# A two-layer Mamba-2 and attention kernel: decay products one or two steps further on, turned x behind weights, last norm's rows on another queue

## Chip, cores, metric

The kernel runs on one core of one Trainium2 chip. The metric is the device time of one execution in microseconds (us). The core has TensorE (PE, matmuls; PEld is its weight load), VectorE (DVE), ScalarE (ACT), GpSimd (POOL), and SyncE (SP), which here only issues DMAs. Each engine works through its own instructions in the order in which they stand in the program; engines wait for each other by semaphores.

## What is computed

Two layers over 256 tokens of width 2048, in float32: a Mamba-2 (SSD) mixer and a sliding-window attention mixer, each followed by a LayerNorm of `ALPHA * x + mixer(x)`. The parts that the change touches are the SSD's diagonal term, its input, and the last norm:

```python
x_c = (xs * dt[..., None])                          # input, scaled by dt
decay_in = jnp.exp(_segsum(da))
cb = jnp.einsum("bcqgn,bcsgn->bgcqs", c_c, b_c)
y_diag = jnp.einsum("bgcqs,bgrcqs,bcsgrp->bcqgrp", cb, decay_in, x_c)
...
y = (xf - mu) * lax.rsqrt(var + EPS) * g + b        # LayerNorm, rows g and b of each layer
```

There are 64 heads in 8 groups of 8, a state of 128, chunks of 128 tokens; the attention has 32 query heads on 4 shared K/V heads.

## The kernel before, in words

**Weights and matmuls.** A float32 product is made of three matmuls in a reduced type: each weight unit (128 x 2048) is split into a high part `wh` (ScalarE, line 143) and a remainder `wl` (VectorE, line 144), and multiplied with the likewise split input `xH`, `xL` (`mac`, lines 269 to 271; `out_unit`, lines 330 to 332). Units come in halves of 512 KB through five buffers `wr`; `load_half` (line 132) issues the next half on SyncE's queue as soon as a half has been converted. `next_unit` converts some units ahead and then calls `flush`, which runs what `posts` holds.

**PSUM.** Products go to four banks `mm`, used in turn. A bank is free again when VectorE has read it: `xr` (line 337 or 339, adds an output product to the residual), `z` (line 530), `cv` (line 457), `sg` (line 980, attention gate). `ax` names four other banks for small matmuls.

**SSD layer.** Group g takes ten blocks of 128 columns: B, C, four of x, four of z (group 0 in another order). Step `10*g + b` is the place after block b of group g, and a table `plan`, filled by `at(step, function, ...)`, says what is called there. This section runs under a manual schedule: the instructions of each engine stand in the order in which the code issues them. Between the blocks stand the output units of the group before (`OUT_AT`). Per group:

- `load_decay` (SyncE, `rb`), `sum_decay` and `exp_decay` (ScalarE) make the decay tiles `e`, two of 4 heads each, `es[g, 0]` and `es[g, 1]`.
- `cb` computes C·B on TensorE (lines 539, 540), masks it into `cbm` (line 541) and multiplies both halves of `e` by it (line 544). `cbm` has one buffer.
- In group 0, `tr` turns x by TensorE and scales it into `xd` (line 560). In groups 1 to 7, `turn_blocks` turns x by blocks on VectorE into `zt` (line 574), stores it to DRAM by four DMAs (`zd`, line 577); `load_turned` reads it back as `xt` (line 585), and `scale_x` makes `xd` of it (line 593). `zt`, `xt` and the later `yz` share one buffer.
- `ymm` (line 609) multiplies `xd` with `e` on TensorE: `es[g, 0]` in its first half, `es[g, 1]` in its second.

The steps are `cb` at 10g + 4 (group 0: 9; group 1: 16), `turn_blocks` at 10g + 5, `load_turned` at 10g + 6, `scale_x` at 10g + 8, `ymm` at 10g + 9 (group 0: 11).

**Attention layer.** Stages follow `B_ORDER`: ..., gate blocks 3 (`gate_block`, last readers of `x1H` and `x1L`), output stage 2, output stage 3, which is `out_last` and computes the last norm (`done2`). In `attend`, the softmax tile `p` is turned by VectorE, stored to DRAM (`pd`, line 988) and read back as `pT` (line 1048), both on GpSimd's queue; `mask_p` makes `pm` of it (VectorE, line 1055). Here a scheduler orders the instructions of each engine. The last norm's rows `gb2` are put where `x1H` and `x1L` were, and are loaded on GpSimd's queue (lines 1109, 1110), 1 MB each as each row is spread over 128 partitions.

Of the kernel before, what the change touches and what calls it, by code (L numbers as in the profile page):

```python
# [12 lines left out]
ALU = mybir.AluOpType  # L13
AX = mybir.AxisListType

P = 128
# [46 lines left out]
def trunk(ctx: ExitStack, tc: tile.TileContext, A: dict, out: bass.AP, dbg=None):  # L63
    nc = tc.nc
# [16 lines left out]
    def nm(s):  # L81
        uid[0] += 1
        return f"{s}_{uid[0]}"
# [4 lines left out]
    def ax_tile():  # L88
        return ax_ps.tile([P, 512], F32, tag="ax", name=nm("ax"), bufs=4)
# [152 lines left out]
    posts = []  # L242

    def flush():
        fns, posts[:] = list(posts), []
        for fn in fns:
            fn()
# [221 lines left out]
    es = {}  # L469
# [42 lines left out]
    gs = [G() for _ in range(NG)]  # L512
# [20 lines left out]
    def cb(g):  # L533
        if g == 0:
            flush()
        st = gs[g]
        cbm = ap.tile([P, 384], F32, tag="cbm", name=nm("cbm"), bufs=1)
        ps = ax_tile()
        nc.tensor.matmul(ps[:, :256], st.bt[:, :128], st.ct[:], start=True, stop=True)
        nc.tensor.matmul(ps[:, 256:384], st.bt[:, 128:], st.ct[:, 128:], start=True, stop=True)  # L540
        nc.vector.tensor_tensor(cbm[:], ps[:, :384], mask_ssd, ALU.mult)
        for hf in range(2):
            e = es[g, hf]
            nc.vector.tensor_tensor(
                e[:], e[:], cbm[:].unsqueeze(1).to_broadcast([P, 4, 384]), ALU.mult
            )

    def tr(g):

# [17 lines left out]
    def turn_blocks(g):  # L567

        flush()
        st = gs[g]  # L570
        zt = ap.tile([P, 4, 2, 4, 32], F32, tag="yz", name=nm("zt"), bufs=1)
        xv = st.xs[:].rearrange("p i (c b t) -> p c b i t", c=2, b=4)
        for c in range(2):
            nc.vector.transpose(zt[:, :, c, :, :], xv[:, c, :, :, :])
        st.zd = dram.tile([4, P, 256], F32, tag="zd", name=nm("zd"), bufs=2)
        for a in range(4):
            nc.sync.dma_start(
                st.zd[a, :, :].rearrange("(b t) f -> t b f", b=4),
                zt[32 * a : 32 * a + 32, :, :, :, :].rearrange("p b c i d -> p b (c i d)"),
            )  # L580

    def load_turned(g):
        st = gs[g]
        st.xt = ap.tile([P, 2, 2, 8, 32], F32, tag="yz", name=nm("xt"), bufs=1)
        nc.sync.dma_start(st.xt[:].rearrange("p r a k d -> p (r a) (k d)"), st.zd[:].rearrange("a p f -> p a f"))

    def scale_x(g):

# [165 lines left out]
    def at(t, fn, *a):  # L754
        plan.setdefault(t, []).append((fn, *a))
# [3 lines left out]
    for g in range(NG):  # L759
        t = 10 * g  # L760
        if g == 0:
            at(3, dts.end)
            at(TD, dts.turn)
            at(TD, load_decay, 0, 1)
            at(TD, load_low, 0)
            steps = TS
            pos = dict(cb=CB0, tr=10, y=11, norm=16)
        elif g == 1:
            at(10, load_decay, 1, 0)
            at(10, load_decay, 1, 1)  # L770
            at(13, load_low, 1)
            steps = 13
            pos = dict(cb=6, zt=ZT_AT, ld=LD_AT, xd=XD_AT, y=Y_AT, norm=10 + CB_AT)
        else:
            at(t - 5, load_decay, g, 0)
            at(t - 5, load_decay, g, 1)
            at(t, load_low, g)
            steps = t - 1
            pos = dict(cb=CB_AT, zt=ZT_AT, ld=LD_AT, xd=XD_AT, y=Y_AT, norm=10 + CB_AT)
        at(steps, sum_decay, g, 0)  # L780
        at(steps + 1, exp_decay, g, 0)
        at(steps + 1, sum_decay, g, 1)
        at(steps + 2, exp_decay, g, 1)
        at(t + pos["cb"], cb, g)
        if g == 0:
            at(t + pos["tr"], tr, g)
        else:
            at(t + pos["zt"], turn_blocks, g)
            at(t + pos["ld"], load_turned, g)
            at(t + pos["xd"], scale_x, g)  # L790
        at(t + pos["y"], ymm, g)
        at(t + pos["y"], gate, g)
        at(t + pos["y"] + 2, split_y, g)
        at(t + pos["norm"], norm, g)
# [311 lines left out]
    x1_stack.close()  # L1106
    gp = pool("gp", side="right")
    gb2 = [gp.tile([P, D], F32, tag=f"gb{i}", name=f"gb2_{i}") for i in range(2)]
    nc.gpsimd.dma_start(gb2[0][:], A["lng"][1].partition_broadcast(P))
    nc.gpsimd.dma_start(gb2[1][:], A["lnb"][1].partition_broadcast(P))  # L1110
    st2 = bp.tile([P, 2, 4, 6], F32, tag="st", name="st2")

    def done2(h):
# [131 lines left out]
```

## Time and profile before

| What | Value |
|---|---|
| Median of 3 runs | 990.82 us (990.53 to 991.11) |
| The profiled execution's own time | 993.6 us |
| Its span, first to last instruction | 991.8 us |
| Mean granted TensorE clock | 0.994 |
| DMA, over the span | 218.72 MB, mean 221 GB/s |
| Weight loads `wr` on SyncE's queue | 322 of 512 KB |

A row of the timeline gives the start in us, the duration, the engine, the line, the operation, the tiles (out<-in) and a count of merged instructions; in brackets stands the idle time of the engine before it, and what ended it. A granted clock of 0.50 means that TensorE runs at half rate.

### The profile page before, as it was taken

The page shows a single profiled execution, that of the slowest core. Times are in us where ns is not written, and L with a number is a line of the kernel's source. Part 1 is how long each engine was busy: PE and PEld are TensorE (multiplying, and loading weights), DVE is VectorE, ACT ScalarE, POOL GpSimd, SP SyncE. Part 2 cuts the span into 40 slices and gives each one's busy share as a digit, 9 for nine tenths or more (in the row PEclk, how much of TensorE's full clock was granted, in tenths as well). Part 3 has the DMA queues.
Part 4 walks back from the last instruction along what each step waited for, and adds up shares of the span by engine and source line. Part 5 has one row for each costly group of instructions (what it writes and reads, how often), then busy time and mean ns, then how long its engine had stood idle before and what let it go on. Part 6 is the DMA issues. An engine that isn't in the chain of part 4 may idle for free.

```text
span 991.8 us, 17619 instructions
## 1 busy us (share of the span) xinstructions
PE 980.7 (99%) x6868; PEld 881.7 (89%) x6868; DVE 795.7 (80%) x1227; ACT 534.5 (54%) x905; POOL 170.1 (17%) x225
## 2 busy tenths in 40 slices
PE   9999999999999999999999999999999999999997
PEld 7999989999998998999999999877898888878875
DVE  6879887976987887796797697999658687878686
ACT  6586747455644835744745554444446454635432
POOL 0004004005046002200400400500202222221102
PEclk9999999999999999999999999999999999999998
DMA  9588885686585666658558657646774849584932
GB/s 367 178 281 271 253 290 153 187 298 174 172 306 178 209 197 242 203 183 308 151 186 304 170 171 261 241 147 218 226 234 140 313 153 327 166 305 119 340 115 86
DMA packets 69443, 218.72 MB, mean 221 GB/s; under 512 B 8096, under 2 KB 19632, under 8 KB 68592
## 3 DMA queue, kind: packets, MB, share of 16 engines
q1 hardware_dynamic: 63648, 198.95, 61.5%
q0 software_dynamic: 5424, 18.12, 5.4%
q8 instruction: 54, 0.88, 0.4%
q10 hardware_dynamic: 288, 0.52, 0.1%
q14 instruction: 29, 0.24, 0.1%
HBM read 205.37 MB, written 12.19 MB: 219 GB/s over the span
## 4 chain that ended last, share of the span: by engine, by line
PE 78%; DVE 11%; ACT 4%; DMA 4%; issue 3%; POOL 0%; DVEq 0%; SPq 0%; POOLq 0%; ACTq 0%
PE mm L269 14%; PE mm L270 14%; PE mm L271 14%; PE mm L330 7%; PE mm L331 7%; PE mm L332 7%; PE mm L881 3%; DVE wl L144 3%; PE mm L882 3%; PE mm L883 3%; PE ax L609 2%; ACT wh L143 1%; DMA pd<-z 1%; PE ax L1007 1%; DMA gb<-in_lng 1%
## 5 line engine op out<-in xcount | busy, mean ns | idle before, releaser
L144 DVE TENSOR_TENSOR wl<-wr,wh 128x1024 fp32r<-128x1024 f32 (+2 forms) x338 | 398.6, 1209 | 92.7 <-ACT wh L143 91.8
L143 ACT ACTIVATE wh<-wr 128x1024 fp32r<-128x1024 f32 (+2 forms) x338 | 328.9, 1012 | 197.1 <-PE mm L331 71.7
L269 PE MATMUL mm<-xH,wh 128*128 128x256 f32 x1280 | 356.2, 278 | 0.0
L270 PE MATMUL mm<-xL,wh 128*128 128x256 f32 x1280 | 355.2, 278 | 0.0
L271 PE MATMUL mm<-xH,wl 128*128 128x256 f32 x1280 | 354.9, 277 | 0.0
L269 PEld LDWEIGHTS mm<-xH,wh 128*128 128x128 f32 x1280 | 240.8, 188 | 3.5 <-issue 0.9
L270 PEld LDWEIGHTS mm<-xL,wh 128*128 128x128 f32 x1280 | 240.8, 188 | 1.0
L271 PEld LDWEIGHTS mm<-xH,wl 128*128 128x128 f32 x1280 | 240.7, 188 | 0.0
L626 POOL TENSOR_TENSOR yz<-yz,z 128x256 f32<-128x256 f32 x32 | 33.3, 1060 | 437.6 <-DVE yz L620 431.5
L330 PE MATMUL mm<-wh,yH 128*128 128x512 f32 x256 | 101.4, 396 | 1.9 <-DVE xr L337 1.9
L331 PE MATMUL mm<-wh,yL 128*128 128x512 f32 x256 | 100.0, 391 | 0.0
L332 PE MATMUL mm<-wl,yH 128*128 128x512 f32 x256 | 99.8, 390 | 0.0
L457 DVE SCALAR_TENSOR_TENSOR cv<-mm,pc,cv 128x255 f32<-128x255 f32 x144 | 69.2, 481 | 15.3 <-ACT cv L455 11.8
L270 PE MATMUL mm<-x1L,wh 128*128 128x256 f32 x256 | 70.9, 277 | 0.0
L269 PE MATMUL mm<-x1H,wh 128*128 128x256 f32 x256 | 70.8, 277 | 0.0
L271 PE MATMUL mm<-x1H,wl 128*128 128x256 f32 x256 | 70.8, 277 | 0.0
L881 PE MATMUL mm<-wh,x1H 128*128 128x512 f32 x160 | 63.8, 398 | 0.0
L883 PE MATMUL mm<-wl,x1H 128*128 128x512 f32 x160 | 62.8, 392 | 0.3 <-DVE wl L144 0.2
L882 PE MATMUL mm<-wh,x1L 128*128 128x512 f32 x160 | 62.7, 392 | 0.2 <-DVE x1L L845 0.2
L455 ACT ACTIVATE cv<-mm,pc 128x256 f32<-128x256 f32 x48 | 26.8, 558 | 63.6 <-PE mm L271 63.5
L330 PEld LDWEIGHTS mm<-wh,yH 128*128 128x128 f32 x256 | 48.1, 188 | 12.5 <-DVE xr L337 2.3
L332 PEld LDWEIGHTS mm<-wl,yH 128*128 128x128 f32 x256 | 48.1, 188 | 10.1
(222 smaller groups left out, 1378.7 us busy)
## 6 DMA issues: line engine op xcount, KB each, us to landing
wr<-in_wa SPq DMA_DIRECT2D x154, 512.0 KB, 5.3
wr<-in_wo SPq DMA_DIRECT2D x64, 512.0 KB, 5.1
wr<-in_wq SPq DMA_DIRECT2D x32, 512.0 KB, 5.1
wr<-in_wg SPq DMA_DIRECT2D x32, 512.0 KB, 5.4
wr<-in_wb SPq DMA_DIRECT2D x32, 512.0 KB, 5.3
rb<-rscr SPq DMA_DIRECT2D x16, 512.0 KB, 5.9
el<-rscr SPq DMA_DIRECT2D x16, 256.0 KB, 7.6
wr<-in_wkv SPq DMA_DIRECT2D x8, 512.0 KB, 6.6
```

What stands on the lines that cost most here:

```text
L143: nc.scalar.activation(h[:, sl], raw, AF.Copy)
L144: nc.vector.tensor_tensor(l[:, sl], raw, h[:, sl].bitcast(F32), ALU.subtract)
L269: nc.tensor.matmul(ps, ah, bh, start=first, stop=False)
L270: nc.tensor.matmul(ps, ah, bl, start=False, stop=False)
L271: nc.tensor.matmul(ps, al, bh, start=False, stop=last)
L330: nc.tensor.matmul(ps[:], aH[:, k, hs], u.h[:, ks], start=k == 0, stop=False)
L331: nc.tensor.matmul(ps[:], aL[:, k, hs], u.h[:, ks], start=False, stop=False)
L332: nc.tensor.matmul(ps[:], aH[:, k, hs], u.l[:, ks], start=False, stop=k == 3)
L457: nc.vector.scalar_tensor_tensor(a[:, sft:], ps[:, : S - sft], w(3 - sft), a[:, sft:], ALU.mult, ALU.add)
L881: nc.tensor.matmul(ps[:], x1H[:, kk, hs], u.h[:, ks], start=kk == 0, stop=False)
L882: nc.tensor.matmul(ps[:], x1L[:, kk, hs], u.h[:, ks], start=False, stop=False)
L883: nc.tensor.matmul(ps[:], x1H[:, kk, hs], u.l[:, ks], start=False, stop=kk == KT - 1)
```

## The change

Three edits.

**Decay products.** `cb` no longer multiplies all of `e`; the product has a function of its own, `weigh`. In groups 2 to 7 `cb` calls it for both halves as before, in group 0 for the first half, in group 1 for none. The rest is in the plan: group 0's second half after `tr` (step 10), group 1's halves at steps 17 and 18.

**Turned x.** The stores of `zd` and the load of `xt` are put into `posts`, so they are issued at the end of the next `next_unit`, behind the weight halves which that one loads.

**Last norm's rows.** `gb2` is loaded on SyncE's queue and not on GpSimd's.

```diff
         nc.vector.tensor_tensor(cbm[:], ps[:, :384], mask_ssd, ALU.mult)
-        for hf in range(2):
-            e = es[g, hf]
-            nc.vector.tensor_tensor(
-                e[:], e[:], cbm[:].unsqueeze(1).to_broadcast([P, 4, 384]), ALU.mult
-            )
+        st.cbm = cbm
+        for hf in range(2 if g > 1 else 1 - g):
+            weigh(g, hf)
+
+    def weigh(g, hf):
+        e = es[g, hf]
+        nc.vector.tensor_tensor(
+            e[:], e[:], gs[g].cbm[:].unsqueeze(1).to_broadcast([P, 4, 384]), ALU.mult
+        )
...
         st.zd = dram.tile([4, P, 256], F32, tag="zd", name=nm("zd"), bufs=2)
-        for a in range(4):
-            nc.sync.dma_start(
-                st.zd[a, :, :].rearrange("(b t) f -> t b f", b=4),
-                zt[32 * a : 32 * a + 32, :, :, :, :].rearrange("p b c i d -> p b (c i d)"),
-            )
+
+        def store():
+            for a in range(4):
+                nc.sync.dma_start(
+                    st.zd[a, :, :].rearrange("(b t) f -> t b f", b=4),
+                    zt[32 * a : 32 * a + 32, :, :, :, :].rearrange("p b c i d -> p b (c i d)"),
+                )
+
+        posts.append(store)
...
-        nc.sync.dma_start(st.xt[:].rearrange("p r a k d -> p (r a) (k d)"), st.zd[:].rearrange("a p f -> p a f"))
+        posts.append(lambda: nc.sync.dma_start(
+            st.xt[:].rearrange("p r a k d -> p (r a) (k d)"), st.zd[:].rearrange("a p f -> p a f")
+        ))
...
             at(t + pos["tr"], tr, g)
+            at(t + pos["tr"], weigh, g, 1)
         else:
+            if g == 1:
+                at(17, weigh, g, 0)
+                at(18, weigh, g, 1)
...
-    nc.gpsimd.dma_start(gb2[0][:], A["lng"][1].partition_broadcast(P))
-    nc.gpsimd.dma_start(gb2[1][:], A["lnb"][1].partition_broadcast(P))
+    for t, name in zip(gb2, ("lng", "lnb")):
+        tc.keep_in_program_order(nc.sync.dma_start(t[:], A[name][1].partition_broadcast(P)))
```

TensorE's and ScalarE's orders are the same in both programs. VectorE's changes in two places. The first is group 1, from its mask `cbm` on. Before (names as the program has them, with buffer numbers; `e_1278` and `e_1364` are the two halves of the decay tile):

```order
L541 TENSOR_TENSOR cbm_1532<-ax_1533,cc 128x384
L544 TENSOR_TENSOR e_1278<-e_1278,cbm_1532 128x1536
L544 TENSOR_TENSOR e_1364<-e_1364,cbm_1532 128x1536
L144 TENSOR_TENSOR wl_1542<-wr_1305,wh_1541 128x1024
L144 TENSOR_TENSOR wl_1542<-wr_1377,wh_1541 128x1024
L337 SCALAR_TENSOR_TENSOR xr<-mm_1551,r_1519,xr 128x512
L337 SCALAR_TENSOR_TENSOR xr<-mm_1565,r_1519,xr 128x512
```

VectorE of the changed program at the same place:

```order
L541 TENSOR_TENSOR cbm_1532<-ax_1533,cc 128x384
L144 TENSOR_TENSOR wl_1539<-wr_1305,wh_1538 128x1024
L144 TENSOR_TENSOR wl_1539<-wr_1377,wh_1538 128x1024
L337 SCALAR_TENSOR_TENSOR xr<-mm_1549,r_1519,xr 128x512
L337 SCALAR_TENSOR_TENSOR xr<-mm_1563,r_1519,xr 128x512
L144 TENSOR_TENSOR wl_1578<-wr_1381,wh_1577 128x1024
L144 TENSOR_TENSOR wl_1578<-wr_1454,wh_1577 128x1024
L530 SCALAR_TENSOR_TENSOR z_1636<-z_1636,mm_1587 128x256
L548 TENSOR_TENSOR e_1278<-e_1278,cbm_1532 128x1536
```

The two products stood ahead of the weights and of the two `xr`; now the first stands behind them and the next block's weights and `z`, and the second one block further on, right ahead of `xd`. In group 0 the second product moves in the same manner, from behind the first to behind the four `xd`.

SyncE's queue in group 2, before (`zd` store of the turned x, `xt` its load, `rb` decay rows for the next group, `wr` weight halves):

```order
L577 DMA zd_2418<-zt_2415 32x4x256 x4
L476 DMA rb_2423<-rscr 128x1024
L476 DMA rb_2425<-rscr 128x1024
L132 DMA wr_2431<-in_wa 128x1024
L132 DMA wr_2435<-in_wo 128x1024
L585 DMA xt_2489<-zd_2418 128x4x256
L132 DMA wr_2495<-in_wo 128x1024
L132 DMA wr_2499<-in_wa 128x1024
```

And in the changed program:

```order
L476 DMA rb_2419<-rscr 128x1024
L476 DMA rb_2421<-rscr 128x1024
L132 DMA wr_2427<-in_wa 128x1024
L132 DMA wr_2431<-in_wo 128x1024
L583 DMA zd_2418<-zt_2415 32x4x256 x4
L132 DMA wr_2494<-in_wo 128x1024
L132 DMA wr_2498<-in_wa 128x1024
L593 DMA xt_2489<-zd_2418 128x4x256
```

`zd` and `xt` each stand two weight halves later, and the two `rb` are the first. The other groups from 1 on move likewise.

The end of SyncE's queue in the changed program, where only `gb` is new:

```order
L132 DMA wr_10437<-in_wb 128x1024
L132 DMA wr_10441<-in_wb 128x1024
L1124 DMA gb_0_10607<-in_lng 128x2048
L132 DMA wr_10486<-in_wb 128x1024
L132 DMA wr_10490<-in_wb 128x1024
L1124 DMA gb_1_10608<-in_lnb 128x2048
L132 DMA wr_10533<-in_wb 128x1024
L132 DMA wr_10537<-in_wb 128x1024
L132 DMA wr_10571<-in_wb 128x1024
```

The two `gb` loads stand among the last weight halves; on GpSimd's queue they stood right behind the last `pT`. The first waits for the last gate matmul that reads `x1L`, as before.

## The prediction

> **What bounds the kernel now.** The first view is the page's busy table with its clock row, read against the span.
>
> ```profile
> span 991.8 us, 17619 instructions
> ...
> PE 980.7 (99%) x6868; PEld 881.7 (89%) x6868; DVE 795.7 (80%) x1227; ACT 534.5 (54%) x905; POOL 170.1 (17%) x225
> ...
> PEclk9999999999999999999999999999999999999998
> ```
>
> TensorE is busy for 980.7 of 991.8 us, and the change takes no matmul away and reorders none. So it can win only where TensorE stands still, or runs at a lower clock. The second view is therefore who TensorE waited for (total us, times, longest):
>
> ```profile
> PE mm L330 <- DVE sg L980: 1.9, 1, 1.9
> PE mm L330 <- DVE xr L337: 1.9, 1, 1.9
> ```
>
> These are its two longest waits, one event each, and both are for a PSUM bank that VectorE has not yet emptied. The third view, the timeline (start, us, engine, line), places them: the `xr` one first.
>
> ```profile
> 124.74 0.39 PE L332 MATMUL mm<-wl,yH 128*128 128x512 f32 x1
> 126.99 0.50 PE L330 MATMUL mm<-wh,yH 128*128 128x512 f32 x1 [1.86 <-DVE xr L337]
> 119.99 0.55 DVE L541 TENSOR_TENSOR cbm<-ax,cc 128x384 f32<-128x384 f32 x1
> 120.58 3.43 DVE L544 TENSOR_TENSOR e<-e,cbm 128x1536 f32<-128x1536 f32 x2
> 123.92 2.35 DVE L144 TENSOR_TENSOR wl<-wr,wh 128x1024 fp32r<-128x1024 f32 x2
> 126.19 1.40 DVE L337 SCALAR_TENSOR_TENSOR xr<-mm,r,xr 128x512 f32<-128x512 f32 x2
> 115.46 2.95 ACT L143 ACTIVATE wh<-wr 128x1024 fp32r<-128x1024 f32 x3
> 124.28 0.39 PE L330 MATMUL mm<-wh,yH 128*128 128x512 f32 x1
> 124.51 0.39 PE L331 MATMUL mm<-wh,yL 128*128 128x512 f32 x1
> ```
>
> This is group 1. VectorE goes from one instruction to the next without idle time: the two decay products (3.43), two weight remainders (2.35), and only then the `xr` that empties the bank. Matmuls of this shape start every 0.23 us (124.28, 124.51, 124.74), so the next was due at 124.97 and came at 126.99: **2.0 us lost**. The second wait, near the end of the kernel:
>
> ```profile
> 939.44 0.39 PE L332 MATMUL mm<-wl,oH 128*128 128x512 f32 x1
> 941.78 0.50 PE L330 MATMUL mm<-wh,oH 128*128 128x512 f32 x1 [1.95 <-DVE sg L980]
> 930.79 1.23 DVE L144 TENSOR_TENSOR wl<-wr,wh 128x1024 fp32r<-128x1024 f32 x1 [0.39 <-ACT wh L143]
> 939.03 1.23 DVE L1055 TENSOR_TENSOR pm<-pT,cc 128x1024 f32<-128x1024 f32 x1 [7.02 <-DMA gb<-in_lng]
> 940.17 1.22 DVE L144 TENSOR_TENSOR wl<-wr,wh 128x1024 fp32r<-128x1024 f32 x1
> 941.31 0.41 DVE L980 SCALAR_TENSOR_TENSOR sg<-sg,mm 128x256 f32<-128x256 f32 x1
> 930.03 0.76 POOL L1048 DMA_DIRECT2D pT<-pd  x1 [6.26 <-DMA pd<-z]
> 930.78 0.55 POOL L1109 DMA_DIRECT2D gb<-in_lng  x1
> 931.32 0.55 POOL L1110 DMA_DIRECT2D gb<-in_lnb  x1
> ```
>
> VectorE stands for 7.02 us before `pm`, which needs the turned softmax tile `pT`. The gate `sg` that empties TensorE's bank is two instructions behind it. TensorE was due at 939.67 and came at 941.78: **2.1 us lost**. The releaser is printed as a `gb` row, but `pm` reads `pT`, so what is awaited is `pT`'s landing. There is a third loss behind this one, in the table of windows (us, length, busy time and count by engine, PEclk, DMA share, GB/s), cut at 3.41 us:
>
> ```profile
> 938.94:942.35 3.41, 1.46 (x6) 0.87 (x6) 3.32 (x4) 0.76 (x1) 0.00 (x0) 1.00 0.91 376
> 942.35:945.77 3.42, 3.42 (x10) 2.65 (x9) 3.42 (x6) 0.00 (x0) 0.00 (x0) 0.50 0.83 255
> 123.15:126.57 3.42, 1.98 (x9) 1.32 (x7) 3.42 (x4) 1.33 (x2) 0.00 (x0) 1.00 1.03 368
> 126.57:129.98 3.41, 2.99 (x14) 2.50 (x15) 3.41 (x5) 1.06 (x1) 0.00 (x0) 1.00 0.87 276
> ```
>
> After a window in which TensorE was busy for 1.46 of 3.41 us the granted clock is 0.50 for 3.42 us: 3.42 x 0.5 = **1.7 us lost**. After the wait in group 1, with 1.98 of 3.42 us busy, it stays at 1.00. The page "TensorE: Matmul & The Clock Gate" of the Trainium skill (section "Part 1: The HAM clock gate") asks for an idle window of about 3.4 us before half rate, free-running against the kernel; the length agrees with the 3.42 here, but a window that was only 57% idle sufficed, so the measurement decides. By the page alone the 1.7 would not be tied to this wait and the sum below would give 987.5.
>
> **Part 1, products of group 1 one and two steps later.** Ahead of the `xr` at 126.19 stands 3.43 us less. The remainders `wl` need `wh`, and the three `wh` from 115.46 end by 118.41, so nothing else holds them: `xr` moves to about 122.8, its bank is free 0.8 us later as now (126.19 to 126.99), at 123.6, and TensorE wants it at 124.97. The 2.0 us go, with 1.4 to spare. What is late next? Product and weights are the same work, spread: up to the next pair of `xr` VectorE has still 1.7 us (one product) less than before, up to the third pair equally much, while TensorE is 2.0 us earlier. TensorE waits nowhere in that stretch now, so this costs nothing as long as the bank there was free 2 us ahead; I take 0, with 1 us as the upper end.
>
> **Part 2, second product of group 0 behind the transposes.**
>
> ```profile
> 72.22 3.43 DVE L544 TENSOR_TENSOR e<-e,cbm 128x1536 f32<-128x1536 f32 x2
> 79.27 1.41 DVE L560 TENSOR_TENSOR xd<-ax,dtx 128x256 f32<-128x256 f32 x4
> 80.00 2.82 PE L609 MATMUL ax<-e,xd 128*64 128x256 f32 x32
> ```
>
> VectorE's total up to 80.68 (79.27 + 1.41) is unchanged, only the product now ends it instead of `xd`. TensorE's 32 matmuls read the second product in their second half, from 80.00 + 1.41 = 81.4. So the cover is 0.7 us, and no TensorE wait stands here to be gained. Value 0; if the cover fails, the loss is bounded by one product, 1.7 us.
>
> **Part 3, turned x behind weights, groups 1 to 7.**
>
> ```profile
> 204.38 0.83 SPq L585 DMA_DIRECT2D xt<-zd  x1
> 205.26 0.80 SPq L132 DMA_DIRECT2D wr<-in_wo  x1
> DMA to landing us min/median/max: 9.7/9.7/9.7
> 217.93 1.29 DVE L593 TENSOR_TENSOR xd<-xt,dtx 128x512 f32<-128x512 f32 x2
> 227.43 0.42 DVE L530 SCALAR_TENSOR_TENSOR z<-z,mm 128x256 f32<-128x256 f32 x1 [2.35 <-ACT z L529]
> ```
>
> Group 2 (the landing row is that of the issue at 204.38): `xt` lands at 214.1 and is read at 217.93, so 3.8 us are to spare, and VectorE has another 2.35 us idle at 227. The store `zd` and the load `xt` each pass two weight loads, and the two `rb` loads go ahead. A weight issue there is some 1 us apart from the next, and `xt` must still wait until `zd` has landed: I put `xt` about 3 us later, inside 3.8. TensorE waited for nothing in groups 2 to 7, so there is nothing to win: value 0. From below, weights that arrive earlier cannot help an engine that waits for none; from above, see the last rival.
>
> **Part 4, the norm's rows on SyncE's queue.** `gb2[0]` comes behind the weight load of 932.04 and ahead of five more; its wait, for the last gate matmul, was over by 930.78, when GpSimd issued it. The five weights behind are those of the last output units, converted a whole stage ahead of use; were that cover gone, 2 MB ahead of them would cost 2.1 MB / 376 GB/s = 5.6 us. `gb` itself is read only at the end:
>
> ```profile
> L1143 DVE SCALAR_TENSOR_TENSOR t<-xr,mv,gb x4: 746/750/1794, 974.8 to 976.8; 128x512 f32<-128x512 f32 x4
> ```
>
> That is 40 us later: both free. What counts is `pT`, no longer followed by 2 MB on its queue. To close the wait whole, it must land 2.1 us earlier, 6.8 us after its issue. All eight `pT` loads, then the last one, then the one issued at 882.4, without any `gb` near it:
>
> ```profile
> DMA to landing us min/median/max: 4.4/7.1/9.0
> DMA to landing us min/median/max: 8.9/8.9/8.9
> DMA to landing us min/median/max: 8.1/8.1/8.1
> ```
>
> I choose 7.6, between the median and the row of the like load before it: `pT` lands 1.3 us earlier, 0.8 us of the wait stays. Bounds: 0 (9.0 is the longest, without `gb`) and 2.1 us. A wait of 0.8 us leaves no window half idle, so the 1.7 us of clock go too.
>
> **Sum.** 2.0 + 0 + 0 + 1.3 + 1.7 = 5.0 us. The profiled execution took 993.6 us (span 991.8): it would take 988.6. The runs have a median of 990.82, 2.8 below the profiled one; I take the same 5.0 from it: **985.8 us**. What is not known: whether an unprofiled run has the second wait and the clock drop at the same size.
>
> **Rivals.**
> 1. *`pT` does not come earlier.* Its issue at 930.03 stands ahead of both `gb` on the queue, and 9.0 us was seen without `gb`: the landing may be set by weight traffic, which runs as before. Then only group 1's wait goes: 990.82 - 2.0 = 988.8. The Trainium skill's page "DMA: Bandwidth & Descriptors" (sections "Queues, rings and completion order", "Issuing engines are not separate DMA queues") speaks for this one: a ring is consumed in order, and all queues share the same 16 engines. Against it: the DMA share is 0.91 in the window of the wait, after `gb` had started.
> 2. *Both waits go whole, and the end keeps its clock.* 2.0 + 2.1 + 1.7 = 5.8, and the last four matmuls, at half clock in the window that ends the program, gain up to some 1 us if the clock drops later: 984.0.
> 3. *The waits come back elsewhere*: the spread products hold a later bank, `pT` stays late: 990.8.
> 4. *Slower.* If `xt` lands more than 3.8 + 2.35 = 6.2 us later than now, VectorE holds up the next banks in groups 2 to 7. At 8 us later: 6 x 1.8 = 10.8 us, less the 5.0: 996.6. Against it: only two weights and one store stand ahead.
>
> **How the numbers follow.** Forecast 0.47 (984.5 to 987.3), rival 1 0.22, rival 2 0.16, rival 3 0.10, rival 4 0.05. A measurement of this kernel tells 0.2%, 2.0 us, from no change, so the borders are 988.8 and 992.8; rival 1 lies on the border and is split. Faster: 0.47 + 0.16 + 0.11 = 0.74; same: 0.11 + 0.10 = 0.21; slower 0.05. The range 983.6 to 989.2 leaves out rivals 3 and 4.
>
> **What would show it.** No TensorE wait for `xr` near 125, nor in the next 20 us; the wait for `sg` under 1 us; PEclk 1.00 in every window from 900 to 970; `pT`'s last landing near 7.6 us; no idle time of VectorE ahead of the L603 `xd` rows. A `pT` of 9 us shows rival 1; idle time ended by `xt` there shows rival 4. The number is wrong most easily if the unprofiled runs never had the drop in clock.

## The result, and the profile after

| What | Before | After |
|---|---|---|
| Median of 8 and 8 runs on the same chip | 990.4 us (988.8 to 992.0) | 986.65 us (985.3 to 988.6) |
| Ratio, 95% interval | | 0.9968 (0.9959 to 0.9978) |
| Span of the profiled execution | 991.8 us | 985.5 us |
| Its mean granted clock | 0.994 | 0.998 |

The changed kernel is faster by 0.32%, that is 3.2 us (2.2 to 4.1); the two medians themselves lie 3.75 us apart. Its page begins with the span, the busy times, and the clock row.

```profile
span 985.5 us, 17642 instructions
...
PE 977.8 (99%) x6868; PEld 879.7 (89%) x6868; DVE 796.8 (81%) x1227; ACT 534.2 (54%) x905; POOL 167.9 (17%) x223
...
PEclk9999999999999999999999999999999999999999
```

The span is 6.3 us shorter than in the profile before, twice what the runs show. Much of that, it will be seen below, belongs to the one execution that was profiled before. The list of TensorE's waits (us in total, times, longest; its first four rows) has lost both of the rows that led it before:

```profile
PE ax L178 <- DVE cc L175: 1.3, 1, 1.3
PE ax L1146 <- ACT dg L1136: 0.9, 1, 0.9
PE mm L269 <- ACT wh L168: 0.3, 1, 0.3
PE ax L853 <- DVE xr L848: 0.3, 1, 0.3
```

Group 1 in the timeline after (start, us, engine, line), VectorE and then TensorE:

```profile
120.76 0.55 DVE L541 TENSOR_TENSOR cbm<-ax,cc 128x384 f32<-128x384 f32 x1
121.23 2.35 DVE L144 TENSOR_TENSOR wl<-wr,wh 128x1024 fp32r<-128x1024 f32 x2
123.50 1.40 DVE L337 SCALAR_TENSOR_TENSOR xr<-mm,r,xr 128x512 f32<-128x512 f32 x2
124.82 2.35 DVE L144 TENSOR_TENSOR wl<-wr,wh 128x1024 fp32r<-128x1024 f32 x2
124.20 0.39 PE L331 MATMUL mm<-wh,yL 128*128 128x512 f32 x1
124.43 0.39 PE L332 MATMUL mm<-wl,yH 128*128 128x512 f32 x1
124.65 0.39 PE L330 MATMUL mm<-wh,yH 128*128 128x512 f32 x1
```

The `xr` follows the weight remainders directly, and TensorE's starts go on at 0.23 us where a hole of 2.25 us was. Nor does TensorE wait later: the list above has nothing for the product `e` or for a bank. The end of the kernel, GpSimd, SyncE's queue and VectorE, and the landing time of that `pT`:

```profile
927.65 0.76 POOL L1062 DMA_DIRECT2D pT<-pd  x1 [6.21 <-DMA pd<-z]
930.05 0.42 SPq L1124 DMA_DIRECT2D gb<-in_lng  x1
938.06 0.37 SPq L1124 DMA_DIRECT2D gb<-in_lnb  x1
933.77 1.23 DVE L1069 TENSOR_TENSOR pm<-pT,cc 128x1024 f32<-128x1024 f32 x1 [4.13 <-DMA pT<-pd]
936.05 0.41 DVE L994 SCALAR_TENSOR_TENSOR sg<-sg,mm 128x256 f32<-128x256 f32 x1
DMA to landing us min/median/max: 6.0/6.0/6.0
```

`pT` lands 6.0 us after its issue, `pm` comes 4.13 us after VectorE went idle (before: 7.02), and `sg` is in time. Last, group 2's turned x (`xd` on VectorE, the issue of `xt` and its landing):

```profile
L603 DVE TENSOR_TENSOR xd<-xt,dtx x2: 682/682/683, 215.1 to 215.7; 128x512 f32<-128x512 f32 x2
L593 SPq DMA_DIRECT2D xt<-zd x1: 377/377/377, 209.2 to 209.2; - x1
DMA to landing us min/median/max: 4.2/4.2/4.2
```

`xt` is issued 4.8 us later (209.2, before 204.38), and lands at 213.4, a little earlier than before (214.1). TensorE is earlier too: counted back from the matmuls that read `xd`, `xt` lands 1.1 us later than before.

### The profile page after: what moved, and what is told of

Same layout as the page of the kernel before. It is cut to its first block, busy times and chain, and to the rows that moved or that the text cites. A ratio compares the mean times of both kernels' runs of the same rounds, so it can differ in the third digit from the quotient of the medians.

```text
span 985.5 us, 17642 instructions
## 1 busy us (share of the span) xinstructions
PE 977.8 (99%) x6868; PEld 879.7 (89%) x6868; DVE 796.8 (81%) x1227; ACT 534.2 (54%) x905; POOL 167.9 (17%) x223
## 4 chain that ended last, share of the span: by engine, by line
PE 96%; DVE 2%; DMA 1%; ACT 0%; issue 0%; SPq 0%
PE mm L269 18%; PE mm L270 18%; PE mm L271 18%; PE mm L330 9%; PE mm L331 9%; PE mm L332 9%; PE mm L895 3%; PE mm L896 3%; PE mm L897 3%; PE ax L619 2%; PE ax L1079 1%; PE ax L1021 1%; DMA first<-in_first 1%; DVE st L823 0%; PE ax L539 0%; DVE t L1157 0%
```

## The experiments

All of them are edits of the kernel before unless said otherwise. A ratio compares runs on the same chip; its interval is 95%.

### Each edit alone

**Products of group 1 alone.** `cb` leaves out group 1's products, and the plan has:

```diff
+            if g == 1:
+                at(17, weigh, g, 0)
+                at(18, weigh, g, 1)
```

> Before with one edit: group 1's two decay products at steps 17 and 18. Theory of parts (each wait is worth its own length): TensorE's 2.0 us wait for xr near 125 goes, nothing else moves, 2.0 us faster than before; the wait for sg near 940 stays as before, with pT landing near 9 us after its issue. Rival, that the whole gain sits here (the sg wait of the profile is not in ordinary runs): 3.7 us faster. Rival, that the wait comes back at a later bank: no change and a new TensorE wait between 127 and 150.

Measured: 987.75 us against 991.07, ratio 0.997 (0.9959 to 0.9982): 3.0 us faster. The interval, 1.8 to 4.1 us, holds both the 2.0 of the theory and the 3.7 of its rival. The wait for `xr` is gone. `sg` causes no wait either, though the norm's rows still follow `pT` on GpSimd's queue; `pT` took 6.5 us here and not the 9 that were expected.

**Rows on SyncE's queue alone.** Only the last two lines of the change's diff.

> Before with one edit: the last norm's rows on SyncE's queue. Theory of parts: pT lands 6 to 7 us after its issue, the sg wait of 2.1 us goes, 1.7 to 2.1 us faster than before; with the drop in clock behind that wait as common as in the profile of before it would be 3.4 to 3.8 us. Rival (pT is set by the weight traffic): pT near 9 us, no change. In both the xr wait near 125 stays at 1.9 us.

Measured: 991.17 us, ratio 1.0005 (0.9996 to 1.0013). `pT` took 5.9 us, there is no wait for `sg` and no half clock near it, the wait for `xr` stays with 2.1 us, and the time is that of before; the interval leaves room for a gain of 0.4 us at most. Neither theory holds: `pT` is shorter, as the first says, and yet the 1.7 to 2.1 us are not there to be won. So in ordinary runs this edit removes nothing that shows.

**Turned x behind weights alone.** Only the `posts` lines of the change's diff.

> Before with one edit: zd and xt behind weights. Theory of parts: TensorE waits for nothing in groups 2 to 7, no change in time (within 0.1%); xt is issued some 5 us later but lands at about the same time, because less stands ahead of it in its queue; VectorE's xd rows come 2 us earlier relative to TensorE as weights land earlier. Rival: it carries part of the change's gain, 0.5 us or more faster, through the xr wait near 125.

Measured: 990.65 us, ratio 0.9997 (0.9986 to 1.0008). Nothing, as its cover said. `xt` landed 5.3 us after its issue (median; 8.9 before). In groups 2 to 6 `xd` starts 10.1 us ahead of the matmuls that read it, 0 to 1.1 us more than before, and not the 2 us more that were expected. `pT`, with the rows behind it, took 7.1 us and `sg` cost 0.4 us, without a drop of the clock.

**Product of group 0 alone.** `cb` leaves out the second half in group 0, and `at(t + pos["tr"], weigh, g, 1)` is added.

> The kernel before with only group 0's second product moved behind the four xd. Theory A (cover of 0.7 us, at most the 0.3 to 0.5 us wait of ymm for xd near 80 that some profiles show goes): time within 0.5 us of before, the wait for xr near 125 stays with 1.7 to 2.1 us, no wait of line L613's ymm for xd. Rival (the product now ends too late for the second half of ymm): a TensorE wait for e of up to 1.7 us near 82, and the time up to 1.7 us above before.

Measured: 991.17 us against 991.08, ratio 1.0007 (0.9995 to 1.0018). No wait for `e` or `xd`, so the cover of 0.7 us holds. Kernels without this edit show, in five of ten profiles, a TensorE wait for `xd` of 0.2 to 0.5 us near 80; none of the four with it does. That is too little to see in the times.

**All but turned x.** The changed kernel with the `zd` and `xt` lines of before.

> The changed kernel without its second edit: turned x is stored and loaded ahead of the weights again, the products and the norm's rows as in the changed kernel. Theory A (that edit has cover on both sides and is worth nothing, and the gain over the products alone is noise): ratio to before 0.9965 to 0.9975, so 987 to 988, xt lands 7 to 10 us after its issue, no wait for it. Rival (the edit gives some 0.5 to 1 us by weights that arrive earlier): 988 to 989, and a small TensorE wait in groups 2 to 7.

Measured: 985.81 us against 989.67, ratio 0.9966 (0.9955 to 0.9978), as the whole change. `xt` lands 9.0 us after its issue (median), no engine waits for it.

**The changed kernel again**, in one series with the first three.

> The changed kernel again, beside the single edits on the same chip: 3.2 to 4.2 us faster than before; the sum of the single edits, if they do not act on each other. No TensorE wait near 125 or 940 in its profile. The spread between its runs is explained by the mean granted clock of each run: 0.997 runs some 2 us longer than 0.999 runs.

Measured: 987.19 us, ratio 0.9963 (0.9949 to 0.9977), without a wait for `xr` or `sg`. The spread between its runs does not follow the mean clock as expected: the slowest two, 988.6 us, have 0.997 and 0.995, but the fastest two, 986.2 and 986.4, have 0.997 as well.

### How often does the second wait occur?

Two more profiles of the kernel before, unchanged.

> The kernel before, unchanged, profiled a second time. Theory A (the wait for the gate near 940 and the half-clock window behind it were a chance of the one profiled execution): the last pT lands 6 to 7.5 us after its issue, TensorE's wait for sg is under 1 us, no window between 930 and 960 is at 0.50, and the wait for xr near 125 is there again with 1.8 to 2.0 us. Theory B (they belong to the kernel before): pT lands near 8.9 us, the wait is near 2 us and a window of 3.4 us at 0.50 follows it.

> The kernel before, unchanged, profiled a third time. Theory A (the wait for sg near 940 is a matter of when pT happens to land): pT lands 5.5 to 7.5 us after its issue and the wait is under 1 us, with no half-clock window there; the wait for xr near 125 is there with about 2 us, with or without a half-clock window behind it. Theory B (the wait for sg is the usual case and the second profile was the exception): pT near 9 us, the wait near 2 us.

Measured: 989.42 and 991.53 us. The first rows of TensorE's waits and `pT`'s landing, first of the second profile, then of the third:

```profile
PE mm L330 <- DVE xr L337: 1.7, 1, 1.7
PE ax L178 <- DVE cc L175: 1.3, 1, 1.3
...
DMA to landing us min/median/max: 6.8/6.8/6.8
```

```profile
PE mm L330 <- DVE xr L337: 2.0, 1, 2.0
PE ax L178 <- DVE cc L175: 1.3, 1, 1.3
...
DMA to landing us min/median/max: 7.1/7.1/7.1
```

The wait for `xr` is there both times; the one for `sg` and the half clock behind it are in neither. The third profile has a half-clock window elsewhere, though (start and end, length, busy time and count of PE, PEld, DVE, ACT, POOL, PEclk, DMA share, GB/s):

```profile
124.75:128.16 3.41, 1.44 (x7) 0.90 (x6) 3.41 (x5) 2.17 (x3) 0.00 (x0) 1.00 0.98 356
128.16:131.58 3.42, 3.42 (x9) 2.67 (x9) 3.42 (x5) 1.02 (x2) 0.00 (x0) 0.50 0.84 280
```

This is right behind the wait of group 1. The kernel with group 0's product alone shows the same:

```profile
124.27:127.68 3.41, 1.49 (x7) 0.94 (x6) 3.41 (x5) 2.04 (x3) 0.00 (x0) 1.00 1.04 372
127.68:131.10 3.42, 3.42 (x9) 2.67 (x8) 3.42 (x4) 1.15 (x2) 0.00 (x0) 0.50 0.80 284
```

The other profiles with this wait don't. In the kernel with turned x alone, the clock's steps (laid out back from its drop at the end, in steps of 3.413 us) cut it so:

```profile
124.11:127.53 3.42, 1.58 (x8) 1.00 (x6) 3.42 (x5) 1.27 (x3) 0.00 (x0) 1.00 0.36 119
127.53:130.94 3.41, 3.41 (x18) 2.91 (x19) 3.41 (x5) 1.06 (x1) 0.00 (x0) 1.00 0.89 282
```

The wait is about as long in all of them (1.7 to 2.1 us); what differs is where the steps of the clock fall on it. With 1.49 of 3.41 us busy the clock halves, with 1.58 it doesn't. Of eight profiles with the wait of group 1 unshortened, two have the drop.

### What a wait costs when it is there

**A late `pT`.** The last `pT` is loaded twice:

```diff
-            nc.gpsimd.dma_start(t[:].rearrange(...), held["d"][:].rearrange(...))
+            for _ in range(2 if (j, h) == (3, 1) else 1):
+                nc.gpsimd.dma_start(t[:].rearrange(...), held["d"][:].rearrange(...))
```

> The kernel before with the last pT loaded twice into the same tile, the second load issued when the first has landed. It prices a late pT. Theory A (the landing of pT decides, from some 6.8 us after the issue on, 8.0 here since one weight remainder now stands behind the gate): pT lands 13 to 15 us after the first issue, TensorE waits 5 to 7 us for sg, a window at 0.50 follows, and the time is 5 to 9 us above the kernel before. Rival (other work fills the place, the wait in the profile of before was not of pT's making): the time is within 2 us of before.

Measured: 993.27 us against 989.67, ratio 1.0035 (1.0018 to 1.0053): 3.4 us slower (1.8 to 5.2), in single runs up to 995.9. That is less than the 5 to 9 us expected. VectorE, TensorE, and the windows behind:

```profile
941.30 1.23 DVE L1058 TENSOR_TENSOR pm<-pT,cc 128x1024 f32<-128x1024 f32 x1 [9.77 <-DMA pT<-pd]
942.91 0.79 PE L330 MATMUL mm<-wh,oH 128*128 128x512 f32 x1 [2.73 <-DVE sg L980]
938.77:942.18 3.41, 1.42 (x7) 0.83 (x5) 0.88 (x1) 0.00 (x0) 0.12 (x1) 1.00 0.88 351
942.18:945.59 3.41, 2.68 (x6) 2.15 (x7) 3.41 (x5) 0.00 (x0) 0.00 (x0) 0.50 0.99 412
945.59:949.01 3.42, 3.42 (x9) 1.95 (x9) 3.42 (x5) 0.92 (x2) 0.00 (x0) 0.50 0.81 274
```

The second load took only 4.1 us, so `pT` landed at 941.11, 11.1 us after the first issue and not 13 to 15. That is 3.1 us past the 8.0 named; TensorE, due at 940.03 and come at 942.91, lost 2.9, and the clock 6.83 x 0.5 = 3.4 us more in this execution. So the mechanism of the second wait stands as predicted: a late `pT` does hold TensorE, and the clock does follow. But of the eight profiles with a single load and the rows right behind it, only the first shows it at this size; that of turned x alone shows 0.4 us, and the other six nothing.

**Half the edit of group 1.** Only the second product moves, to step 17.

> The kernel before with only the second product of group 1 moved, to step 17; the first stays ahead of the weights. Theory A (the order on VectorE alone makes the wait for xr, us for us): xr comes 1.7 us earlier, the wait shrinks from 2.1 to 0.4 us, TensorE's starts behind it come 1.7 us earlier, and the time is 1.7 us (0.17%) below before. Theory B (any relief of that stretch is enough, or the gain of group 1 is a matter of the clock and not of the wait): the whole 2.2 to 3 us, or nothing.

Measured: 987.29 us against 989.67, ratio 0.9975 (0.9965 to 0.9985): 2.5 us (1.5 to 3.5). TensorE at the place:

```profile
124.90 0.39 PE L332 MATMUL mm<-wl,yH 128*128 128x512 f32 x1
125.34 0.50 PE L330 MATMUL mm<-wh,yH 128*128 128x512 f32 x1
```

The hole is 0.44 us, 0.2 more than the usual step. From matmul 906 to matmul 1000 (counted from 0), 17.67 us before, TensorE took 1.8 us less here and 2.15 us less in the changed kernel. The time does not tell the theories apart (1.7 us, or 2.2 to 3), but these starts do: the order on VectorE sets the wait, us for us. One product moved would have been nearly enough.

**One product more in group 1.** An instruction of the same size, which changes no value, stands behind the two products:

```diff
+            if g == 1 and hf == 1:
+                nc.vector.tensor_tensor(e[:], e[:], e[:], ALU.max)
```

> The kernel before with one more instruction of a product's size behind group 1's two products (the maximum of e with itself, 128x1536, about 1.7 us; values unchanged). It makes the wait for xr longer. Theory A (the price of that wait is its length, and besides, where it empties more than half of one 3.41 us window of the clock, 1.7 us at half clock; a longer wait does that in nearly every run): the wait grows from 2.1 to 3.8 us, a window at 0.50 stands behind it in the profile, the mean clock of the runs falls by 0.001 to 0.0015, and the time is 2.7 to 3.5 us above before. Theory B (the wait costs its length alone): 1.7 us above before, clock as before.

Measured: 993.94 us against 991.39, ratio 1.002 (1.0008 to 1.0033): 2.0 us (0.8 to 3.3). The wait, and the windows around it:

```profile
PE mm L330 <- DVE xr L337: 3.9, 1, 3.9
...
126.95:130.36 3.41, 0.00 (x0) 0.00 (x0) 3.41 (x5) 2.33 (x3) 0.00 (x0) 1.00 0.60 206
130.36:133.77 3.41, 3.33 (x8) 2.66 (x9) 3.41 (x6) 1.06 (x1) 0.00 (x0) 0.50 0.83 286
```

The wait grew by 2.0 to 4.1 us (hole of 4.32 less 0.23), and the half-clock window is there: for theory A, but in one execution. The time, with both theories inside its interval, decides nothing. The mean clock of the runs fell from 0.9969 to 0.9948, and that is no clean witness. One half-clock window is 0.0017 of the mean (3.41 x 0.5 of 990 us), so the fall is more than this window can give; and the mean also counts the kernel's end, where the profiles show 1.2 to 8.7 us at half clock.

### What makes pT's load long

The rows stay on GpSimd's queue, but are issued some 29 us later, at 959.5 and 960.0:

```diff
-    nc.gpsimd.dma_start(gb2[0][:], A["lng"][1].partition_broadcast(P))
-    nc.gpsimd.dma_start(gb2[1][:], A["lnb"][1].partition_broadcast(P))
+    late = bp.tile([P, 2], F32, tag="late", name="late")
+    nc.gpsimd.tensor_copy(late[:, 0:1], xr[:, 1, D - 1 :])
+    for t, name in zip(gb2, ("lng", "lnb")):
+        nc.gpsimd.tensor_copy(t[:, 0:1], late[:, 0:1])
+        nc.gpsimd.dma_start(t[:], A[name][1].partition_broadcast(P))
```

> The kernel before with the norm's rows still on GpSimd's queue, but issued only when the output before has been stored, behind small copies that wait for it; two one-column copies are added. Theory A (what lengthens pT's load is the 2 MB in flight beside it, and not the queue they stand in): pT lands 5.4 to 6.1 us after its issue, as with the rows on SyncE's queue, there is no wait for sg, and the time is within 1 us of before, the wait for xr near 125 still there. Theory B (its landing is set by weights alone): 6.5 to 9 us as with the rows behind it. Rival for the time: rows that land too late for the last norm make the end 1 to 3 us longer.

Measured: 990.5 us against 991.08, ratio 1.0 (0.999 to 1.001); `pT` took 5.8 us, and the end was not longer. This one profile fits theory A, and the other profiles with and without rows behind the last `pT` lean the same way:

| Rows | `pT` landed after its issue, us |
|---|---|
| right behind it on its queue, 8 profiles | 8.9, 7.8, 7.2, 7.1, 7.1, 6.8, 6.5, 5.7; mean 7.1 |
| on SyncE's queue, or later, 5 profiles | 6.0, 5.9, 5.8, 5.7, 5.4; mean 5.8 |

The two groups overlap in one value, so the size of the effect, some 1.4 us, is rough. That the rows' bytes and not their queue do it rests on the one profile with late rows.

The length of the load is also only half of what decides. Let the time at which TensorE wants the bank of `sg` be the last start ahead of that matmul plus 0.23 us. Counted back from there, the last `pT` was issued 9.0 to 12.6 us ahead in the fourteen profiles. What counts is how far ahead it landed, since `sg` was done some 2.8 us after the landing (938.95 to 941.72 in the first profile):

| Profile | `pT` issued ahead, us | Load, us | Landed ahead, us | TensorE lost, us |
|---|---|---|---|---|
| before, the first | 9.6 | 8.9 | 0.7 | 2.1 |
| turned x alone | 9.4 | 7.1 | 2.3 | 0.5 |
| products of group 1 alone | 9.4 | 6.5 | 2.9 | 0 |
| before, the third | 10.1 | 7.1 | 3.0 | 0 |
| half the edit of group 1 | 12.6 | 7.8 | 4.8 | 0 |

A load of 7.1 us cost TensorE 0.5 us in one execution and nothing in another, and one of 7.8 us cost nothing at all.

## Why the prediction was right, and where not

985.8 us was predicted and 986.65 measured, inside the range and inside the forecast's own range. But two terms of the sum were sized by a single execution, and the gain was 3.2 us (2.2 to 4.1), not 5.0.

- **Part 1, 2.0 us: right.** 2.15 us by TensorE's starts, in the changed kernel and in the kernel with these products alone; no later bank was late. What the term lacked is the clock, which had stayed at 1.00 in the one execution it was read from: its wait, too, halves the clock in some executions (two of eight profiles). At 1.7 us each that is 0.4 us a run, an estimate from few profiles. 2.15 + 0.4 = 2.6 lies inside every interval measured for kernels with both products moved; the 0.4 to 1.1 us up to their centers (3.0 to 3.7) are not explained. One place to look is the kernel's end: from matmul 6860 to the last (6867) TensorE took 4.3 to 5.2 us in the four profiles with both products moved (mean 4.7) and 4.5 to 5.6 in the ten others (mean 5.4), by how half clock falls there. Whether that is more than the luck of four profiles is open.
- **Part 2, 0: right.** The cover of 0.7 us held. That there was nothing to gain is not quite so: the wait for `xd` of 0.2 to 0.5 us in some profiles seems to have been there to be won, since no profile with the edit has it.
- **Part 3, 0: right.** In group 2, 1.7 us lie between the landing and `xd` (213.4 to 215.1) where 3.8 lay before: against `xd` on VectorE, which reads it, `xt` comes 2.1 us later, for 3 predicted. But the cover was worked out for group 2 alone. In group 7 it is used up: there VectorE makes `xd` as soon as `xt` lands, and in the second profile of the changed kernel it stood idle for 1.35 us until then, the idle time that the prediction named as a sign against it. TensorE read that `xd` only 3.2 us after the landing, and so lost nothing.
- **Part 4, 1.3 + 1.7 = 3.0 us: wrong for ordinary runs, and the mis-sized step.** "`pT` lands 1.3 us earlier" was right in kind (7.1 to 5.8 us on the mean, though 7.6 was named). The bound "6.8 us after its issue" belongs to an execution in which `pT` was issued 9.6 us ahead, and is not fixed. And the 2.1 us wait it was to shorten, and the 1.7 us of clock behind it, were a chance of that one execution, in which `pT` took 8.9 us. None of the other seven profiles with the rows behind `pT` and the load left single has a wait for `sg` over 0.4 us, and the rows alone gave 1.0005. The prediction had named this ("whether an unprofiled run has the second wait and the clock drop at the same size") without pricing it.
- **Why the number came out close all the same.** The sum was taken from the median, 2.8 us below the profiled execution, but its terms from that execution. The 2.8 us were in large part these very terms: from matmul 6400 to 6800 (897 to 967 us) that execution took 4.5 us longer than the second and the third profile of the same kernel. So in the runs part 4's 3.0 us were missing, and 985.8 is still only 0.85 us off, because three things made up for 2.15 of them: the 990.82 of three runs lay 0.4 us above the median of the eight that stood beside the changed kernel, the medians lie 0.55 us further apart than the ratio says, and the rest of the change was worth 3.2 us and not 2.0. That is luck, but for the 0.6 us by which part 1 can be seen to be worth more.
- **The rivals.** No wait came back elsewhere, and nothing became slower through `xt`. Rival 1's reason (a `pT` that comes no earlier) doesn't hold on the mean, though its outcome, that only group 1's wait counts, does; its 988.8 us, with that wait at 2.0, was too slow for the runs (985.3 to 988.6). Rival 2's picture, both waits gone whole, is what the profile after shows beside the profile before. As a statement on the runs, at 984.0 us, it fails like part 4.

## What to carry to other kernels

Where the profiled execution is slower than every ordinary run shown, ask which of its waits are the difference before taking a gain from them: a wait that hangs on a DMA's landing differs from run to run, one that hangs on the order of an engine's instructions is there each time. Profile the unchanged kernel a second time, and sum only what both show. A stall of some 2 us is best priced as its length plus the chance that it leaves one of the clock's windows less than 45% busy (some 1.5 of 3.41 us), times the 1.7 us that such a window costs.

## What the hardware showed unexpectedly

- The clock's windows are 3.413 us long: in the third profile of the kernel before, the clock drops at 128.16 and again, at the kernel's end, at 981.50 us, and these 853.34 us are 250 such steps. They stand in each execution at another place against the program. A window with TensorE busy for 1.42 to 1.49 us of it was followed by half clock (four profiles), one with 1.58 us was not. So it takes no full idle window, and the same 2.0 us stall costs 2.0 or 3.7 us by chance.
- Busy time of matmuls with one row of weights seems not to count. At the end of the changed kernel a window with 2.52 us busy, 1.98 of them in four matmuls with one row of weights, was followed by half clock as well (the matmuls, then the windows):

```profile
974.97 1.98 PE L1135 MATMUL ax<-gb,cc 1*128 1x512 f32 x4
...
974.84:978.25 3.41, 2.52 (x6) 0.96 (x6) 3.24 (x7) 0.90 (x3) 1.24 (x2) 1.00 0.51 191
978.25:981.66 3.41, 3.00 (x4) 0.67 (x2) 2.70 (x5) 0.96 (x2) 0.00 (x0) 0.50 0.16 61
```

Laid out in such steps through all fourteen profiles, with the one-row matmuls left out, every window at full clock that was followed by half clock had 0 to 1.49 us busy (25 windows), and every one followed by full clock had 1.58 us or more. With them counted in, windows of up to 3.3 us busy were followed by half clock, and the rule fails.
- At half clock, a window with 2.68 us busy was followed by a second one at half clock (the late `pT`, above); windows with 3.00, 3.33 and 3.42 us busy were followed by full clock. Over the fourteen profiles, 1.0 to 2.8 us busy kept it at half, and 2.85 us or more brought it back.
- `xt`, issued behind two weight loads more, took 4.5 us from its issue to its landing in place of 8.9 (medians over groups 1 to 7, the changed kernel and the one before). Counted back from the matmuls that read `xd`, it was issued 5.7 to 6.6 us later in groups 2 to 6, and landed only 1.1 to 2.1 us later. Most of the earlier issue won nothing here.
